# Due times that count each engine's queue, rests of splits written over the loaded tiles, and shorter pauses between the first operands of the up projection

## The chip, the cores and the metric

The kernel runs on one core of a Trainium2 chip. The metric is the device time of one execution in microseconds, as the median of several runs; lower is better. Five parts of the core matter here: TensorE (PE, matrix products and transposes by products with an identity), VectorE (DVE), ScalarE (ACT), the SyncE queue (SP) that hands out the transfers, and the DMA engines. GpSimd (POOL) does next to nothing.

## The reference

One layer of a decoder in fp32, for 2048 positions of 1024 features: two parallel groups of heads, cross-attention into 256 memory tokens, a gated feed-forward part, and norms between.

```python
h = rms_norm(x, mix_norm_g);  z = h @ w_in                      # 1024 -> 2048
lru_x, lru_gate, conf_a, conf_b = split(z, 4)
lru_x = causal_dwconv(lru_x, lru_conv_w, lru_conv_b)            # 4 taps
y_lru = rg_lru(lru_x, ...) * gelu(lru_gate)                     # gates, then a scan along positions
c = causal_dwconv(conf_a * sigmoid(conf_b), conf_conv_w, conf_conv_b)   # 31 taps
c = silu(layer_norm(c, conf_ln_g, conf_ln_b))
x = x + concat([y_lru, c]) @ w_out
h = rms_norm(x, xa_norm_g);  m = rms_norm(mem, mem_norm_g)
p = softmax((h @ w_q) . (m @ w_k) / 16)                         # 4 heads of 256
x = x + (p @ (m @ w_v)) @ w_o
h = rms_norm(x, ffn_norm_g);  g, u = split(h @ w_up, 2)         # 1024 -> 2 x 3072
x = x + (gelu(causal_dwconv(g, ffn_conv_w, ffn_conv_b)) * u) @ w_down
return rms_norm(x, final_norm_g)
```

## The kernel before

**Products.** Each fp32 operand of a product is split into two rounded parts: `hi`, a copy in a rounded format (ACT), and `lo`, the rest (DVE subtracts `hi` from the source). `mm3` (L603) then makes three matmuls of a 128x128 by 128x512 tile: hi by hi, lo by hi, hi by lo. The names in the profile are `xh/xl`, `yh/yl`, `Xh/Xl`, `hidh/hidl` and `wh/wl`. Larger products are made from seven block products in place of eight, with sums and differences of blocks (`S1` to `S4` on one side, `T1` to `T4` on the other): `seven` (L1129) with weights that `Quads` (L1078) prepares for the mixer's and attention's output products, `strassen_cols` (L1450) for the up projection, whose activations `HalfX` (L1388) holds, and `Down` (L1582 on) for the down projection, with weights from `prepare_down`.

**Stages.** Up to about 550 us: norms, memory, input projection and the convolutions. About 550 to 1090 us: for each half of the positions (`attend`, L1273) the recurrent gates, the product with w_out, attention (scores, exponentials of `prob`, transposes of it into `pt`, product into the residual `x1`), and the norm before the feed-forward part. From about 1090 us: the up projection, first for the positions of half 0, then (about 1550 us) half 1; then the down projection and the last norm.

**What sets the order.** Nothing is issued as it is written. The parts of the layer are generators; `drive` (L510) steps them by a clock that counts the recorded PE work, and a `yield n` pauses a generator for n us of that clock. They record operations (`Program.do`, `Program.dma`, L199 and L227), each with an engine, an estimated cost, predecessors, and the buffers that it touches. Tiles come from pools of slots: 85 of 128x512 (`S`), 4 and 3 wider ones, 8 banks of PSUM (`ps`), and a tile gets its slot when an earlier one has been let go. When all is recorded, `emit` (L403) plans up to three times: `deadlines` (L260) gives each operation a due time from an order of PE's work, and `schedule` (L281) walks through time, and on each engine issues, of the operations that are ready, the one with the earliest due time. The next pass takes its PE order from the last; the plan with the shortest estimate is issued, engine by engine, each engine in its planned order.

A due time before is that of the PE work behind it less the costs and hops of the chain between:

```python
for o in reversed(self.ops):
    lat = o.cost + o.delay + HOP
    for s in o.succs:
        o.due = min(o.due, s.due - lat)
```

It counts the chain of one operation, not what else stands on the engine. In a split, `lo` has its own slot (`pair`, L499; `split`, L595). `first_x` (L1785 on) makes the first four operands of the up projection, `X[0].make(key)`, with a pause of 20 behind each, and `feed_forward` starts when it has ended.

Of the kernel before, what the change touches and what calls it, by code (L numbers as in the profile page):

```python
# [11 lines left out]
F32 = mybir.dt.float32  # L12
# [5 lines left out]
P = 128  # L18
# [38 lines left out]
PASSES = 3  # L57

# [11 lines left out]
class Buf:  # L70


    def __init__(self, tag, shape, real=None, dtype=F32, name="t"):
        self.tag, self.shape, self.real, self.dtype, self.name = tag, tuple(shape), real, dtype, name
        self.ops, self.heads = [], []
# [24 lines left out]
class Ref:  # L100
    def __init__(self, buf, steps, dummy):
        self.buf, self.steps, self.dummy = buf, steps, dummy

    def __getitem__(self, i):
        return Ref(self.buf, self.steps + (lambda ap: ap[i],), self.dummy[i])

    def f32(self):
        return Ref(self.buf, self.steps + (lambda ap: ap.bitcast(F32),), self.dummy)
# [22 lines left out]
def resolve(a):  # L131
    return a.resolve() if isinstance(a, Ref) else a

# [13 lines left out]
class Program:  # L147
# [51 lines left out]
    def do(self, eng, name, out, *args, reads=(), writes=(), **kw):  # L199
        outs = [out] + ([kw["accum_out"]] if "accum_out" in kw else [])  # L200
        ins = [a for a in list(args) + list(kw.values()) if isinstance(a, Ref) and a not in outs]
        if eng == "PE":
            o = self.group or self.op("PE")
            n = ins[1].n if name == "matmul" else P
            if name == "matmul":
                rounded = ins[1].buf.dtype == F32R
                cost = (n + 32) / 2400.0 if rounded else n * 4 / 2400.0
            else:
                cost = 0.11
# [11 lines left out]
        o.calls.append((name, (out,) + args, kw))  # L221
        self.touch(
# [37 lines left out]
    def deadlines(self, order):  # L260
# [10 lines left out]
        for o in reversed(self.ops):  # L271
# [6 lines left out]
            if o.first:  # L278
                o.due = o.idx - 1e6

# [167 lines left out]
def hybrid_layer(  # L448
# [629 lines left out]
    class Quads:  # L1078
# [7 lines left out]
        def prepare(self, pace):  # L1086
            sub = ALU.subtract
            for i in range(KH):
# [5 lines left out]
                for n, t in enumerate((b11, b21, t2, t1, t3, t4, b22)):  # L1094
                    for j, b in enumerate(parts(t)):
# [30 lines left out]

    held = [0]

    def seven(order, L, W, add, amid):  # L1129
        banks, left = {}, {}  # L1130
# [4 lines left out]
        for n, (p, bank, start, outs) in enumerate(order):  # L1135
# [4 lines left out]
            for i in range(KH):  # L1140
                lh, ll = parts(L.get(akey, i))
# [246 lines left out]
    class HalfX:  # L1388
# [40 lines left out]
        def make(self, key):  # L1429
            sub = ALU.subtract  # L1430
            if key in self.t:
# [13 lines left out]
            for b in src:  # L1445
                hi, lo = pair("X")
                split(b[:], hi, lo)
                self.B[key].append((hi, lo))

    def strassen_cols(c0, B, outs, used=None):  # L1450
# [11 lines left out]
        def product(bank, src, key, start):  # L1462
            X = B.get(key)
            wh, wl = pair("w", (P, KQ, P))
            split(src, wh, wl)
# [25 lines left out]
        product(c, s1[:], "T1", True)  # L1491
        yield 0
        s3 = comb(a11, a21, ALU.subtract)
        product(a, s3[:], "T3", False)
# [8 lines left out]
        product(c, s4[:], "B22", False)  # L1503
# [54 lines left out]
    def prepare_down():  # L1558
        yield attends[NH - 1]
        for c in range(NCK):  # L1560
            for i in range(KD):
                f = c * 2 * KD + i
                raw = []
                for r0 in (f * P, (f + KD) * P):
                    for half in range(2):
                        t = tmp("wd")
                        pr.dma(t[:], w_down[0, r0 : r0 + P, half * TT : (half + 1) * TT])
                        raw.append(t[:])
                b11, b12, b21, b22 = raw
                t1 = combine("t", b12, b11, ALU.subtract)  # L1570
                t2 = combine("t", b22, t1[:], ALU.subtract)
                t3 = combine("t", b22, b12, ALU.subtract)
                t4 = combine("t", b21, t2[:], ALU.subtract)
# [236 lines left out]
```

## Time and profile before

| | |
|---|---|
| time, median of 3 runs | 2493.47 us (2490.45 to 2495.44) |
| the profiled execution | 2495.1 us |
| its span | 2493.3 us |
| its mean granted clock of TensorE | 0.988 |
| matmuls and transposes on PE | 10788 |
| ACT in the page | 2256 instructions |
| DMA | 572.07 MB, 229 GB/s over the span |

The time is that of the whole execution; the span runs from the first to the last instruction of the profile. All instructions are issued from one line of the recorder (L420, in the changed kernel L447), so that groups and rows are told apart by the names of their tiles, `out<-in`. A row of the timeline is start, duration, engine, line, operation, tiles and shape, a count `xN` where like rows follow each other, and in brackets how long the engine had been idle and what ended it. Durations of neighbours overlap: instructions are pipelined, so the pitch from start to start is what one costs.

### The profile page before, as it was taken

How to read it: one execution, taken by the hardware profiler on the slowest of the kernel's cores; microseconds unless marked ns; L12 is line 12 of the kernel's file. 1: busy time of each engine (PE TensorE's matmuls, PEld its weight loads, DVE VectorE, ACT ScalarE, POOL GpSimd, SP SyncE). 2: the span in 40 equal slices, each digit the busy share in tenths (PEclk: the TensorE clock that was granted, in tenths of full speed). 3: DMA queues.
4: the chain of work that ended last, by engine and by line, in shares of the span. 5: the costliest groups of instructions: out<-in, count | busy, mean ns of one | idle time of the engine just before them, and what ended most of it. 6: DMA issues, size and time to landing. Idle time of an engine off the chain costs nothing.

```text
span 2493.3 us, 32519 instructions
## 1 busy us (share of the span) xinstructions
PE 2421.8 (97%) x10788; PEld 1988.5 (80%) x10788; DVE 1921.3 (77%) x3187; ACT 1290.6 (52%) x2256; POOL 0.7 (0%) x6
## 2 busy tenths in 40 slices
PE   6999999999998999999999999999999999999998
PEld 5788868877767888878888887788888888888886
DVE  4579968999988645779888887987876775667665
ACT  8426668266977655775545455654443431233222
POOL 0000000000000000000000000000000000000000
PEclk8999999999999999999999999999999999999999
DMA  6987678797786966586654546644422288769774
GB/s 221 376 296 228 228 237 302 248 349 243 241 300 224 372 221 228 167 278 241 226 204 155 182 162 194 235 166 163 169 76 85 93 293 269 249 224 368 257 251 157
DMA packets 339839, 572.07 MB, mean 229 GB/s; under 512 B 32925, under 2 KB 106653, under 8 KB 339671
## 3 DMA queue, kind: packets, MB, share of 16 engines
q1 hardware_dynamic: 339670, 570.00, 67.0%
q8 instruction: 85, 1.39, 0.2%
q14 instruction: 84, 0.68, 0.1%
HBM read 385.32 MB, written 184.55 MB: 229 GB/s over the span
## 4 chain that ended last, share of the span: by engine, by line
PE 87%; DVE 5%; DMA 4%; ACT 3%; issue 1%; SPq 0%; DVEq 0%; ACTq 0%
PE ps L420 87%; ACT prob L420 1%; DVE yl L420 1%; DMA raw<-in_w_out_dram 1%; DVE t L420 1%; DMA VO<-VO 0%; DMA x<-in_x_dram 0%; DMA yf<-yf 0%; DVE s L420 0%; DVE prob L420 0%; DVE xc L420 0%; DVE gate L420 0%; ACT L420 0%; DVE Xl L420 0%; ACT x L420 0%
## 5 line engine op out<-in xcount | busy, mean ns | idle before, releaser
L420 PE MATMUL ps<-Xh,wl 128*128 128x512 f32 x1344 | 523.9, 390 | 2.5 <-DVE wl L420 2.5
L420 PE MATMUL ps<-Xh,wh 128*128 128x512 f32 x1344 | 524.3, 390 | 1.6 <-ACT wh L420 1.6
L420 PE MATMUL ps<-Xl,wh 128*128 128x512 f32 x1344 | 523.4, 389 | 0.0
L420 PEld LDWEIGHTS ps<-Xh,wl 128*128 128x128 f32 x1344 | 252.6, 188 | 57.1 <-DVE wl L420 4.7
L420 PEld LDWEIGHTS ps<-Xh,wh 128*128 128x128 f32 x1344 | 252.7, 188 | 55.3 <-ACT wh L420 2.9
L420 PEld LDWEIGHTS ps<-Xl,wh 128*128 128x128 f32 x1344 | 252.7, 188 | 52.1
L420 PE MATMUL ps<-wh,yh 128*128 128x512 f32 x672 | 268.9, 400 | 7.0 <-ACT pt L420 3.7
L420 PE MATMUL ps<-wh,yl 128*128 128x512 f32 x672 | 265.0, 394 | 4.9 <-DVE yl L420 4.9
L420 PE MATMUL ps<-wl,yh 128*128 128x512 f32 x672 | 264.5, 394 | 0.1
L420 PE MATMUL ps<-wh,hidh 128*128 128x512 f32 x672 | 261.4, 389 | 0.0
L420 PE MATMUL ps<-wl,hidh 128*128 128x512 f32 x672 | 261.4, 389 | 0.0
L420 PE MATMUL ps<-wh,hidl 128*128 128x512 f32 x672 | 261.4, 389 | 0.0
L420 DVE TENSOR_TENSOR acc<-acc,ps 128x512 f32<-128x512 f32 x192 | 129.5, 685 | 150.3 <-PE ps L420 149.9
L420 PE MATMUL ps<-xh,wh 128*128 128x512 f32 x512 | 201.8, 394 | 0.9 <-DMA wh<-w_in 0.8
L420 PE MATMUL ps<-xh,wl 128*128 128x512 f32 x512 | 199.5, 390 | 2.3 <-DVE wl L420 1.7
L420 PE MATMUL ps<-xl,wh 128*128 128x512 f32 x512 | 199.3, 389 | 0.0
L420 ACT ACTIVATE wh<-s 128x512 fp32r<-128x512 f32 x192 | 119.8, 629 | 136.5 <-DVE s L420 99.9
L420 PEld LDWEIGHTS ps<-wh,yh 128*128 128x128 f32 x672 | 128.0, 191 | 36.9 <-ACT pt L420 4.6
L420 PEld LDWEIGHTS ps<-wh,yl 128*128 128x128 f32 x672 | 127.9, 190 | 34.1 <-DVE yl L420 7.1
L420 DVE TENSOR_TENSOR wl<-s,wh 128x512 fp32r<-128x512 f32 x192 | 131.2, 688 | 27.3 <-ACT wh L420 25.4
L420 ACT ACTIVATE u<-ps 128x512 f32<-128x512 f32 x144 | 85.9, 597 | 126.5 <-PE ps L420 125.4
L420 PEld LDWEIGHTS ps<-wl,yh 128*128 128x128 f32 x672 | 128.2, 191 | 27.6 <-issue 0.8
(200 smaller groups left out, 4113.0 us busy)
## 6 DMA issues: line engine op xcount, KB each, us to landing
raw<-in_w_up_dram SPq DMA_DIRECT2D x96, 512.0 KB
wh<-w_down SPq DMA_DIRECT2D x164, 256.0 KB
wl<-w_down SPq DMA_DIRECT2D x164, 256.0 KB
hid<-cv SPq DMA_DIRECT2D x48, 512.0 KB
h<-hid SPq DMA_DIRECT2D x96, 256.0 KB
w_down<-wh SPq DMA_DIRECT2D x84, 256.0 KB
w_down<-wl SPq DMA_DIRECT2D x84, 256.0 KB
x<-in_x_dram SPq DMA_DIRECT2D x64, 256.0 KB
```

The lines of the kernel that those rows point to most:

```text
L420: getattr(e, name)(*[resolve(a) for a in args], **{k: resolve(a) for k, a in kw.items()})
```

## The change

Three parts, and no instruction of PE, DVE or SP is added or removed; ACT has three more table loads, since its functions stand in another order.

1. `deadlines` runs over each of DVE, ACT and SP twice (`STACKS`) behind the chain's due times: from the latest due operation of the engine back to the earliest, each is due no later than the next one's due time less its own cost, so that operations that compete for an engine push each other forward; then the chain's rule carries this to the predecessors.

2. A new `split_over` writes `lo` over the source tile itself, in place of a slot of its own. It does so where the source was written only by transfers or already rounded (`loaded`), and where the source isn't read any more; else it takes a slot as before. In `seven` the last uses are counted out by `last_uses`. In the profile such a rest reads as `raw<-raw,yh` where it read `yl<-raw,yh`.

3. `first_x` pauses for 5 in place of 20.

```diff
+STACKS = 2
...
+class Over:
+    def __init__(self, buf):
+        self.buf, self.dtype = buf, F32R
+    def __getitem__(self, i):
+        return self.buf[i].r()
...
         o.calls.append((name, (out,) + args, kw))
+        for r in outs:
+            if not r.rounded:
+                r.buf.loaded = False
...
             if o.first:
                 o.due = o.idx - 1e6
+        for _ in range(STACKS):
+            for e in ("DVE", "ACT", "SP"):
+                t = 1e9
+                for o in sorted((o for o in self.ops if o.eng == e and not o.first), key=lambda o: -o.due):
+                    t = o.due = min(o.due, t - o.cost)
+            for o in reversed(self.ops):
+                lat = o.cost + o.delay + HOP
+                if o.eng != "PE" and not o.first:
+                    for s in o.succs:
+                        o.due = min(o.due, s.due - lat)
...
+    def split_over(b, name):
+        hi, lo = rnd(name + "h", b.shape), Over(b) if b.loaded else rnd(name + "l", b.shape)
+        ACT(hi[:], b[:], AF.Copy)
+        V("tensor_tensor", lo[:], b[:], hi[:].f32(), op=ALU.subtract)
+        return hi, lo
...
-                    for j, b in enumerate(parts(t)):
+                    for j, b in enumerate(split_over(t, "y")):
...
-                lh, ll = parts(L.get(akey, i))
+                lh, ll = split_over(L.get(akey, i), "y") if n in spent else parts(L.get(akey, i))
...
-                hi, lo = pair("X")
-                split(b[:], hi, lo)
+                if self.h or key[0] == "T" or key == "B22":
+                    hi, lo = split_over(b, "X")
+                else:
+                    hi, lo = pair("X")
+                    split(b[:], hi, lo)
...
-        product(c, s1[:], "T1", True)
+        product(c, None, "T1", True, s1)
...
-                    hi, lo = pair("w")
-                    split(src, hi, lo)
+                    hi, lo = split_over(src, "w")
...
-                hi, lo = pair("hid")
-                split(src[:], hi, lo)
+                if akey in ("S1", "S3", "S4") or (akey == "A22" and not self.h):
+                    hi, lo = split_over(src, "hid")
+                else:
+                    hi, lo = pair("hid")
+                    split(src[:], hi, lo)
...
         for key in UP_ORDER[:EARLY]:
             X[0].make(key)
-            yield 20
+            yield 5
```

How this moves instructions is shown at three places.

DVE in the input projection, around 100 us; `wl<-raw,wh` is the rest of a tile of w_in that PE is to use next, `sg` the evacuation of its products, and `t` and `yl` are differences and rests of w_out, stored for much later. Before:

```order
L420 TENSOR_TENSOR yl<-t,yh 128x512
L420 TENSOR_TENSOR t<-raw 128x512
L420 TENSOR_TENSOR t<-raw,t 128x512
L420 TENSOR_TENSOR sg<-ps,sg 128x512
L420 TENSOR_TENSOR t<-raw,t 128x512
L420 TENSOR_TENSOR yl<-t,yh 128x512 x2
L420 TENSOR_TENSOR sg<-ps,sg 128x512
L420 TENSOR_TENSOR yl<-t,yh 128x512
L420 TENSOR_TENSOR yl<-raw,yh 128x512
L420 TENSOR_TENSOR wl<-raw,wh 128x512 x5
```

The changed kernel, at the same `sg` rows:

```order
L447 TENSOR_TENSOR yl<-t,yh 128x512
L447 TENSOR_TENSOR t<-raw,t 128x512
L447 TENSOR_TENSOR t<-raw 128x512
L447 TENSOR_TENSOR t<-raw,t 128x512
L447 TENSOR_TENSOR yl<-t,yh 128x512
L447 TENSOR_TENSOR raw<-raw,yh 128x512 x2
L447 TENSOR_TENSOR yl<-t,yh 128x512 x2
L447 TENSOR_TENSOR sg<-ps,sg 128x512 x3
L447 TENSOR_TENSOR wl<-raw,wh 128x512 x2
L447 TENSOR_TENSOR sg<-ps,sg 128x512
L447 TENSOR_TENSOR wl<-raw,wh 128x512 x2
```

Before, the `wl` rows stand behind the last `yl`; after, they follow the `sg` rows, and the `yl` and `t` rows between the `sg` rows have gone ahead of them or behind.

ACT at the first softmax, around 685 us; `prob,small<-prob,small` are the exponentials with their sums, `yh<-s` splits of the w_out product's left side. Before:

```order
L420 ACT_TABLE_LOAD
L420 ACTIVATE m<-m 128x512
L420 ACTIVATE yh<-s 128x512 x3
L420 ACT_TABLE_LOAD
L420 ACTIVATE prob,small_125<-prob,small_124,small_118 128x256
L420 ACTIVATE prob,small_128<-prob,small_127,small_118 128x256
L420 ACTIVATE prob,small_131<-prob,small_130,small_118 128x256
L420 ACTIVATE prob,small_134<-prob,small_133,small_118 128x256
L420 ACTIVATE prob,small_125<-prob,small_124,small_118 128x256
L420 ACTIVATE prob,small_128<-prob,small_127,small_118 128x256
L420 ACTIVATE prob,small_131<-prob,small_130,small_118 128x256
L420 ACTIVATE prob,small_134<-prob,small_133,small_118 128x256
```

The changed kernel:

```order
L447 ACT_TABLE_LOAD
L447 ACTIVATE m<-m 128x512
L447 ACT_TABLE_LOAD
L447 ACTIVATE prob,small_134<-prob,small_133,small_118 128x256
L447 ACTIVATE prob,small_131<-prob,small_130,small_118 128x256
L447 ACTIVATE prob,small_128<-prob,small_127,small_118 128x256
L447 ACTIVATE prob,small_125<-prob,small_124,small_118 128x256
L447 ACTIVATE prob,small_134<-prob,small_133,small_118 128x256
L447 ACTIVATE prob,small_131<-prob,small_130,small_118 128x256
L447 ACTIVATE prob,small_128<-prob,small_127,small_118 128x256
L447 ACTIVATE prob,small_125<-prob,small_124,small_118 128x256
L447 ACTIVATE yh<-s 128x512 x2
```

Three `yh<-s` stood between the square roots (`m<-m`) and the exponentials; now there is none, and two stand behind all eight exponentials.

PE at the start of the up projection, around 1088 us; `wh,yl` are the last matmuls of the attention's output, `ident,xn` transposes of the normalised rows of the second half of the positions, `Xh` and `Xl` the activations of the up projection. Before:

```order
L420 MATMUL ps<-wh,yh 128x512
L420 MATMUL ps<-wl,yh 128x512
L420 MATMUL ps<-wh,yl 128x512
L420 MATMUL ps<-ident,xn 128x128 x16
L420 MATMUL ps<-Xh,wh 128x512
L420 MATMUL ps<-Xl,wh 128x512
L420 MATMUL ps<-Xh,wl 128x512
```

The changed kernel:

```order
L447 MATMUL ps<-wh,yh 128x512
L447 MATMUL ps<-wl,yh 128x512
L447 MATMUL ps<-wh,yl 128x512
L447 MATMUL ps<-Xh,wh 128x512
L447 MATMUL ps<-Xl,wh 128x512
L447 MATMUL ps<-Xh,wl 128x512
```

The sixteen transposes are gone from here: 144 matmuls with `Xh` and `Xl` stand ahead of the first eight transposes, and the rest of them come between later products, eight or four at a time. On DVE the differences `t<-xn` and rests `Xl` of the first four operands move forward with them.

SP, not shown, hands out the reloads of w_in (`wh<-w_in`, `wl<-w_in`) around 500 us ahead of some stores of `A`, `z` and `gelu` which stood ahead of them.

More of the change, by code (lines that the diff above doesn't have):

```diff
@@ L74, in __init__ @@
         self.tag, self.shape, self.real, self.dtype, self.name = tag, tuple(shape), real, dtype, name
-        self.ops, self.heads = [], []
+        self.ops, self.heads, self.loaded = [], [], True
         self.free = int(np.prod(self.shape[1:]))
@@ L205, in do @@
             if name == "matmul":
-                rounded = ins[1].buf.dtype == F32R
-                cost = (n + 32) / 2400.0 if rounded else n * 4 / 2400.0
+                cost = (n + 32) / 2400.0 if ins[1].rounded else n * 4 / 2400.0
             else:
@@ L1125, in hybrid_layer, with last_uses, make @@
              ("P7", "a", False, [C21, C22]), ("P2", "a", True, [C11]), ("P3", "b", False, [C12]))
+    NEEDS = dict(S1=("A21", "A22"), S2=("S1", "A11"), S3=("A11", "A21"), S4=("A12", "S2"))
+    def last_uses(keys):
+        made, uses = set(), {}
+        def make(key, n):
+            if key in NEEDS and key not in made:
+                made.add(key)
+                for k in NEEDS[key]:
+                    make(k, n)
+                    uses[k] = n
+        for n, key in enumerate(keys):
+            make(key, n)
+        return [n for n, key in enumerate(keys) if uses.get(key, -1) <= n]
     held = [0]
     def seven(order, L, W, add, amid):
+        spent = last_uses([PRODUCTS[p][0] for p, _, _, _ in order])
         banks, left = {}, {}
@@ L1430, in make @@
             sub = ALU.subtract
+            assert not self.h or self.t or key[0] == "B"
             if key in self.t:
@@ L1460, in comb, with product @@
             return t
-        def product(bank, src, key, start):
+        def product(bank, src, key, start, over=None):
             X = B.get(key)
-            wh, wl = pair("w", (P, KQ, P))
-            split(src, wh, wl)
+            if over:
+                wh, wl = split_over(over, "w")
+            else:
+                wh, wl = pair("w", (P, KQ, P))
+                split(src, wh, wl)
             with together():
@@ L1490, in strassen_cols @@
         c = ps()
-        product(c, s1[:], "T1", True)
+        product(c, None, "T1", True, s1)
         yield 0
         s3 = comb(a11, a21, ALU.subtract)
-        product(a, s3[:], "T3", False)
+        product(a, None, "T3", False, s3)
         u3 = copied(a)
@@ L1502, in strassen_cols @@
         s4 = comb(a12, s2[:], ALU.subtract)
-        product(c, s4[:], "B22", False)
+        product(c, None, "B22", False, s4)
         outs(0, 1, u2, c)
@@ L1567, in prepare_down @@
                         pr.dma(t[:], w_down[0, r0 : r0 + P, half * TT : (half + 1) * TT])
[L1568 removed]
+                        raw.append(t)
                 b11, b12, b21, b22 = raw
[L1570 to L1573, printed above, removed]
[L1574 to L1576 removed]
+                t1 = combine("t", b12[:], b11[:], ALU.subtract)
+                t2 = combine("t", b22[:], t1[:], ALU.subtract)
+                t3 = combine("t", b22[:], b12[:], ALU.subtract)
+                t4 = combine("t", b21[:], t2[:], ALU.subtract)
+                for key, src in (("B11", b11), ("B21", b21), ("T2", t2), ("T1", t1), ("T3", t3), ("T4", t4), ("B22", b22)):
+                    hi, lo = split_over(src, "w")
                     at = wd_at(c, key, i)
```

11 lines of the change are left out of this document (7 added, 4 removed).

## The prediction

> **What bounds the kernel now.** I read the page first, then the table of windows, then PE's waits, then the timeline around each wait.
>
> ```profile
> PE 2421.8 (97%) x10788; PEld 1988.5 (80%) x10788; DVE 1921.3 (77%) x3187; ACT 1290.6 (52%) x2256; POOL 0.7 (0%) x6
> 550.00:600.00 50.00, 46.12 (x201) 36.99 (x200) 50.00 (x87) 30.10 (x49) 0.00 (x0) 0.97 0.81 267
> 650.00:700.00 50.00, 43.53 (x171) 32.38 (x170) 44.17 (x87) 46.29 (x85) 0.00 (x0) 0.90 0.80 268
> 700.00:750.00 50.00, 45.10 (x188) 34.42 (x187) 47.93 (x90) 35.39 (x72) 0.00 (x0) 0.97 0.91 327
> 750.00:800.00 50.00, 43.60 (x191) 35.50 (x190) 47.43 (x80) 41.25 (x88) 0.00 (x0) 0.90 0.63 207
> 1000.00:1050.00 50.00, 47.70 (x229) 39.87 (x228) 36.48 (x76) 39.65 (x98) 0.00 (x0) 0.97 0.54 174
> 1050.00:1100.00 50.00, 44.16 (x189) 36.04 (x188) 37.45 (x65) 31.22 (x68) 0.00 (x0) 0.91 0.83 284
> 1100.00:1150.00 50.00, 49.59 (x241) 41.18 (x241) 41.89 (x68) 38.77 (x65) 0.00 (x0) 0.99 0.63 219
> 1550.00:1600.00 50.00, 46.88 (x201) 36.93 (x200) 50.00 (x80) 35.25 (x59) 0.00 (x0) 1.00 0.74 254
> 1600.00:1650.00 50.00, 50.00 (x222) 41.44 (x221) 46.33 (x74) 26.59 (x41) 0.00 (x0) 1.00 0.56 190
> 2400.00:2450.00 50.00, 50.00 (x223) 41.40 (x222) 34.47 (x55) 12.07 (x21) 0.00 (x0) 1.00 0.72 243
> ```
>
> In a row of windows stand the stretch, then the busy time and count of PE, PEld, DVE, ACT and POOL, the granted clock, the DMA share and GB/s. PE is the bound: 97% busy, and from 1600 us to 2450 it has not one idle tenth (50.00 of 50 at both ends of that stretch, clock 1.00). A full window holds 222 matmuls of 512 columns, so one costs 50/222 = 0.225 us. The change alters no count of matmuls. All that it can win is PE's idle time and the stretches at half clock that follow the longer waits, and both lie before 1600 us. A window's clock of 0.90 is 10% of 50 us lost, 5.0 us; 0.97 is 1.5. Where PE idles DVE is at 44 to 50 of 50, so there a step's place in DVE's queue decides. The slots that the in-place rests free can win nothing after 1600; before it they count only through the order.
>
> ```profile
> PE ps L420 <- ACT prob L420: 6.1, 2, 5.3
> PE ps L420 <- ACT xn L420: 5.4, 1, 5.4
> ...
> PE ps L420 <- DVE sum L420: 4.1, 2, 3.2
> PE ps L420 <- DMA wh<-w_in: 0.8, 1, 0.8
> PE ps L420 <- DMA wl<-w_in: 0.6, 1, 0.6
> ```
>
> The waits are total, count and longest, in us. These and the single waits below are the ones that the new order touches; the others (memory tokens, x and gains at the start) keep their place in it, and the tail behind the last matmul is the same.
>
> **The change part by part.** The in-place rests cost nothing by themselves: the instruction has the same shape, only its output lies elsewhere, and the nearest row of a subtraction into its own input takes as long as one into a new slot:
>
> ```profile
> L420 DVE TENSOR_TENSOR acc<-acc,ps 128x512 f32<-128x512 f32 x192 | 129.5, 685 | 150.3 <-PE ps L420 149.9
> L420 DVE TENSOR_TENSOR wl<-s,wh 128x512 fp32r<-128x512 f32 x192 | 131.2, 688 | 27.3 <-ACT wh L420 25.4
> ```
>
> 685 against 688 ns: nothing. (A later reader of the raw tile could be delayed; none is left, since only its last use writes over it.) What remains is order, in seven places.
>
> (a) Around 105 us, second block of w_in columns.
>
> ```profile
> 102.44 0.69 DVE L420 TENSOR_TENSOR sg<-ps,sg 128x512 f32<-128x512 f32 x1
> 103.05 0.68 DVE L420 TENSOR_TENSOR yl<-t,yh 128x512 fp32r<-128x512 f32 x1
> 103.65 0.68 DVE L420 TENSOR_TENSOR yl<-raw,yh 128x512 fp32r<-128x512 f32 x1
> 104.25 1.89 DVE L420 TENSOR_TENSOR wl<-raw,wh 128x512 fp32r<-128x512 f32 x3
> 104.99 0.50 PE L420 MATMUL ps<-xh,wl 128*128 128x512 f32 x1 [1.72 <-DVE wl L420]
> ```
>
> PE waits 1.72 for a `wl` that stands behind `yl` rows of w_out, which nobody needs for some 2000 matmuls. Two stand between the last `sg` and it (2 x 0.60 = 1.2), more before. In the new order `wl` follows the `sg` rows directly. I take -1.4; bounds 0 (the loaded tile or `wh` is late instead) and -1.7.
>
> (b) Around 503 us SP hands out the w_in reloads 24 matmuls earlier (24 x 0.225 = 5.4 us), past stores of A, z and gelu that nothing waits for soon. The two DMA waits, 0.8 + 0.6, go: -1.4, bounds 0 and -1.4.
>
> (c) 550 to 600 us, recurrent gates and w_out product. Idle 50 - 46.12 = 3.9, clock 1.5. The queues ahead of each late step are as long as before, within one or two rows of 0.60. -1, bounds +1 and -5.4 (all of it).
>
> (d) 640 to 800 us, both softmaxes of the first half. Idle 6.5 + 4.9 + 6.4 = 17.8, clock 5.0 + 1.5 + 5.0 = 11.5.
>
> ```profile
> 685.55 0.79 PE L420 MATMUL ps<-wh,yl 128*128 128x512 f32 x1 [2.99 <-DVE yl L420]
> 685.74 0.60 ACT L420 ACTIVATE prob<-prob,small,small 128x256 f32<-128x256 f32 x1 [1.47 <-DVE small L420]
> 690.43 2.89 ACT L420 ACTIVATE prob<-prob,small 128x256 f32<-128x256 f32 x7
> 753.49 3.35 DVE L420 RECIPROCAL r<-r 128x512 f32<-128x512 f32 x1
> 757.57 4.23 PE L420 MATMUL ps<-ident,prob 128*128 128x128 f32 x16 [5.32 <-ACT prob L420]
> ```
>
> In the first softmax the eight exponentials, 690.43 - 685.74 = 4.7 us of ACT, now stand ahead of the last two `yh<-s` of which the next product needs one at once. They also began before (they waited 1.47 for `small`), so the product slips 3 to 4 us; but the probabilities are then ready when the transposes come, which gives back 0.8 (the wait that stands there now) to 4. In the second softmax the 3.35 us reciprocal `r`, which stood ahead of the four small reciprocals that the 5.32 wait needs, goes behind them, and 24 products stand ahead of the `sum,ones` matmuls that waited 3.2. -2 to -5 there. Net -2; bounds +6 (slips of 4 and 2, nothing back) and -10 (the 5.32 and the 3.2 go, with 1.5 of clock).
>
> (e) 1019 us, a softmax of the second half.
>
> ```profile
> 1016.67 0.60 ACT L420 ACTIVATE prob<-prob,small,small 128x256 f32<-128x256 f32 x1
> 1017.26 0.60 ACT L420 ACTIVATE prob<-prob,small,small 128x256 f32<-128x256 f32 x1
> 1018.42 2.04 ACT L420 ACTIVATE pt<-ps 128x512 f32<-128x512 f32 x4
> 1019.07 0.80 PE L420 MATMUL ps<-wh,yh 128*128 128x512 f32 x1 [2.30 <-ACT pt L420]
> 1019.66 0.63 PE L420 MATMUL ps<-wl,yh 128*128 128x512 f32 x1
> ```
>
> Three exponentials stand ahead of the `pt` copies before, eight after: 5 x (1017.26 - 1016.67) = 2.9 more, less an estimated 1 to 2, since four copies of probabilities (0.4 each) stand further up and ACT comes there earlier. +1 of wait and +1 of clock: +2, bounds 0 and +5 (2.9 and 2 of clock).
>
> (f) 1076 to 1125 us, start of the up projection. This is the largest term.
>
> ```profile
> 1087.52 0.39 PE L420 MATMUL ps<-wh,yl 128*128 128x512 f32 x1
> 1093.34 2.96 PE L420 MATMUL ps<-ident,xn 128*128 128x128 f32 x7 [5.43 <-ACT xn L420]
> 1080.60 3.69 DVE L420 TENSOR_TENSOR t<-xn,t 128x512 f32<-128x512 f32 x6
> ```
>
> Before, 16 transposes of the normalised second half of the positions stand next, and wait for its statistics. With the shorter pause the up projection of the first half is recorded ahead of them, and 144 `X` matmuls (144 x 0.225 = 32.4 us) stand ahead of the transposes. The 5.43, the 0.4 that the window from 1100 lacks, and the clock behind (0.91 and 0.99: 4.5 + 0.5 = 5.0) go: -10.8. What is late next is DVE: from the first `t<-xn` to the last rest `Xl` that the product on T3 needs the order has 59 DVE rows at (1084.21 - 80.60)/6 = 0.60, 35.4 us, against 141 matmuls x 0.225 = 31.7. So 3.7 us come back, spread over the first products. -7.1; bounds -10.8 (DVE has a lead) and -2 (the 3.7 falls in one piece and clocks down again for 5.0).
>
> On that last bound the Trainium skill speaks. The rows at 1019 show half speed right after a wait of only 2.30 us: a matmul of 512 columns takes 0.63 and 0.80 us there, against 0.39 at 1087. "TensorE: Matmul & The Clock Gate", Part 1, has the array fall to half rate after at least one idle window of about 3.4 us. By that rule the pieces here, none above 3.4, would cost no clock, and the bound -2 would be -7; by the row a piece of 2.3 can cost it, so I keep -2.
>
> (g) 1549 to 1566 us, change to the second half of the rows.
>
> ```profile
> 1551.70 0.50 PE L420 MATMUL ps<-Xh,wl 128*128 128x512 f32 x1 [1.35 <-DVE wl L420]
> ```
>
> The window from 1550 lacks 50 - 46.88 = 3.1 us of PE, this 1.35 the longest piece, with DVE at 50.00 of 50. The new order puts each `wl` one product (12 matmuls, 2.7 us) earlier, ahead of the splits of the new half. -2.3, bounds 0 and -3.1.
>
> Three more table loads (75 to 78) cost ACT 3 x 1.28 us, and ACT is 52% busy: nothing on PE, except where they stand inside (d), whose bounds hold one.
>
> ```profile
> 755.14 1.28 ACT L420 ACT_TABLE_LOAD   x1
> 756.43 0.69 ACT L420 ACTIVATE r<-ps,eps 128x512 f32<-128x512 f32 x1
> ```
>
> The page "ScalarE: Activation LUTs", section "What ACT_TABLE_LOAD costs", of the Trainium skill adds a drain of about 1.38 us to each; the next ACTIVATE here starts 0.01 behind the load, so the trace does not show it in front of work; by the page three would be an estimated 8 us of ACT instead of 4.
>
> Sum: -1.4 - 1.4 - 1 - 2 + 2 - 7.1 - 2.3 = -13.2 on the profiled execution's 2495.1 (span 2493.3), that is 2481.9. That execution lies 1.6 above the median of the runs, 2493.5, so on the median: **2480**.
>
> **The rivals.**
> - *The moves cancel* (same). (f) ends at -2, since its DVE backlog falls in one piece, (d) at +4, (c) and (g) at 0 and -1: -1.4 - 1.4 + 0 + 4 + 2 - 2 - 1 = +0.2, 2494. For it: DVE is at its limit wherever PE waits (50.00 of 50), so an earlier step makes another later. Against: (f) and (g) have work moved that has hundreds of matmuls to spare.
> - *Exponentials ahead of operands* (slower). Four softmax blocks each put eight exponentials, 4.7 us of ACT, ahead of a `yh` or `pt`. If all four delay PE in full and one new wait clocks it down (5.0), it is 18.8 + 5.0, less the 13.2 of the other five terms ((d) and (e) cancel in the forecast): +10.6, 2504. It decides from three in full (14.1 + 5.0 - 13.2 = +5.9). For it: the new order at 685 and 1019. Against: half of these exponentials already stood there and PE was waiting anyway.
> - *DVE's backlog dissolves* (larger gain). With (c) at -4 and (d) at -10, the rest as forecast: -24.2, 2469. For it: 21.7 us idle and 13.0 of clock lie there. Against: the number of DVE rows ahead of the late steps there hardly shrinks.
>
> **How the numbers follow.** The forecast has 0.58, the moves that cancel 0.19, the slower case 0.12, the larger gain 0.11. 0.2%, 5.0 us, is about what a measurement of this kernel can tell from no change. Faster is forecast and larger gain, 0.58 + 0.11 = 0.69; same 0.19; slower 0.12. Added as independent, the distances from value to bound give 10 us on each side (mostly (d) with 8 and (f) with 4 to 5): 2470 to 2490. To hold 8 in 10 it is widened to both neighbours, 2468 to 2494, which leaves out the slower case and the ends of the others.
>
> **What would show it.** (a): no `wl` wait at 105. (b): no w_in wait at 503. (d): the 5.3 for `prob` gone, a new `yl` or `yh` wait of 3 to 4 after 680. (e): the wait for `pt` near 1019 at 3 to 4. (f): no wait for `xn`, 1.00 of clock there, and small waits for `Xl` of about 3.7 together. (g): under 1 of `wl` and `wh` waits near 1550. After 1600 windows of 50.00. The prediction is wrong if (f) shows a new long wait, or if PE's idle time between 550 and 800 moves by more than 10.

## The result

| | before | changed |
|---|---|---|
| median | 2493.36 us (2490.45 to 2495.44, 4 runs) | 2479.55 us (2477.32 to 2480.82, 4 runs) |
| profiled execution, its span | 2495.1, 2493.3 | 2480.82, 2479.0 |
| ratio to before, 95% interval | | 0.994 (0.9926 to 0.9954) |

The change is worth 13.8 us on the medians and 14.3 in the profiled spans. (In the experiments below one execution of e5 and one of e9 took some two times as long as the others or more; the medians 2485.42 and 2483.38 include it, and without it are 2484.76 and 2483.16.) The page of the changed kernel has the same matmuls and, but for three more on ACT, the same counts:

```profile
PE 2411.2 (97%) x10788; PEld 1986.0 (80%) x10788; DVE 1915.0 (77%) x3187; ACT 1290.1 (52%) x2259; POOL 0.7 (0%) x6
```

Its windows, in the columns of the prediction's:

```profile
550.00:600.00 50.00, 45.46 (x197) 37.05 (x196) 49.14 (x82) 31.80 (x51) 0.00 (x0) 0.93 0.82 264
650.00:700.00 50.00, 40.35 (x161) 31.44 (x160) 42.92 (x82) 45.17 (x83) 0.00 (x0) 0.90 0.78 261
700.00:750.00 50.00, 41.31 (x181) 32.33 (x180) 45.72 (x85) 35.72 (x83) 0.00 (x0) 0.97 0.95 332
750.00:800.00 50.00, 49.50 (x223) 39.96 (x223) 49.09 (x83) 37.40 (x74) 0.00 (x0) 0.96 0.63 200
1000.00:1050.00 50.00, 46.56 (x218) 38.75 (x217) 32.87 (x63) 33.53 (x77) 0.00 (x0) 0.93 0.55 169
1050.00:1100.00 50.00, 48.69 (x214) 39.68 (x213) 44.18 (x74) 31.10 (x70) 0.00 (x0) 1.00 0.65 225
1100.00:1150.00 50.00, 49.09 (x232) 40.53 (x232) 37.17 (x65) 36.28 (x56) 0.00 (x0) 1.00 0.53 183
1550.00:1600.00 50.00, 50.00 (x220) 41.27 (x221) 50.00 (x83) 31.15 (x54) 0.00 (x0) 1.00 0.62 207
2400.00:2450.00 50.00, 50.00 (x222) 41.44 (x221) 31.36 (x50) 11.79 (x22) 0.00 (x0) 1.00 0.52 179
```

Better: 750, 1050 (clock 0.91 to 1.00) and 1550. Worse: 650 and 700 lost 3 to 4 us of PE time to waits, and 1000. Windows mislead a little here, since the work in them has slid by up to 15 us. PE's waits of the changed kernel (total, count, longest) have other names in front:

```profile
PE ps L447 <- ACT pt L447: 6.9, 3, 3.4
PE ps L447 <- DVE sum L447: 6.0, 1, 6.0
PE ps L447 <- ACT yh L447: 5.0, 2, 3.3
PE ps L447 <- ACT xa L447: 3.5, 1, 3.5
...
PE ps L447 <- DVE Xl L447: 1.2, 1, 1.2
...
PE ps L447 <- DVE gb L447: 0.9, 1, 0.9
...
PE ps L447 <- ACT prob L447: 0.7, 2, 0.5
PE ps L447 <- DVE wl L447: 0.5, 1, 0.5
```

The waits for `xn` (5.4), w_in (1.4) and most of those for `wl` (4.2) and `prob` (6.1) are gone; `pt`, `sum`, `yh` and `xa` have grown by 2 to 4 each.

To compare like with like I cut both traces by PE's matmuls, counted from the first, at counts where both have the same work behind them, and take the time from start to start. That is the loss of a stage with its half clock included, in us:

| stage (matmuls) | before at | before | changed | difference | forecast |
|---|---|---|---|---|---|
| start (to 300) | 0 | 84.7 | 82.9 | -1.8 | 0 |
| a (300 to 1000) | 85 | 158.4 | 156.0 | -2.4 | -1.4 |
| 1000 to 2130 | 243 | 255.3 | 256.5 | +1.1 | 0 |
| b (2130 to 2200) | 498 | 17.9 | 15.9 | -2.0 | -1.4 |
| 2200 to 2400 | 516 | 45.8 | 47.3 | +1.5 | 0 |
| c (2400 to 2650) | 562 | 59.6 | 60.6 | +1.0 | -1 |
| d, first softmax (2650 to 2960) | 622 | 78.3 | 80.4 | +2.1 | } -2 |
| d, second softmax (3080 to 3300) | 727 | 64.6 | 58.9 | -5.7 | } |
| e (4340 to 4500) | 1011 | 36.6 | 39.1 | +2.5 | +2 |
| f (4620 to 5300) | 1075 | 157.4 | 150.1 | -7.3 | -7.1 |
| g (6650 to 6950) | 1538 | 73.7 | 69.3 | -4.4 | -2.3 |
| behind the last matmul | 2482 | 11.4 | 12.5 | +1.1 | 0 |

The stages left out differ by less than 0.05. The column sums to -14.3, the spans' difference.

### The profile page after: what moved, and what is told of

The parts are those of the page before. It is cut to its first block, busy times and chain, and to the rows that moved or that the text cites. A ratio compares the mean times of both kernels' runs of the same rounds, so it can differ in the third digit from the quotient of the medians.

```text
span 2479.0 us, 32376 instructions
## 1 busy us (share of the span) xinstructions
PE 2411.2 (97%) x10788; PEld 1986.0 (80%) x10788; DVE 1915.0 (77%) x3187; ACT 1290.1 (52%) x2259; POOL 0.7 (0%) x6
## 4 chain that ended last, share of the span: by engine, by line
PE 68%; DVE 6%; ACT 3%; DMA 1%; issue 1%; SPq 0%; DVEq 0%; ACTq 0%
PE ps L447 68%; ACT prob L447 2%; DVE yl L447 1%; DVE s L447 1%; DVE t L447 1%; DVE gate L447 0%; DVE x L447 0%; DMA wh<-w_out 0%; DMA VO<-yh 0%; DVE Xl L447 0%; ACT yh L447 0%; DVE small L447 0%; DVE prob L447 0%; DVE xc L447 0%; DVE wl L447 0%
## 5 line engine op out<-in xcount | busy, mean ns | idle before, releaser
L447 PE MATMUL ps<-wh,hidl 128*128 128x512 f32 x624 | 242.7, 389 | 0.0
L447 PE MATMUL ps<-Xl,wh 128*128 128x512 f32 x576 | 224.3, 389 | 1.3 <-DVE Xl L447 1.2
L447 ACT ACTIVATE wh<-raw 128x512 fp32r<-128x512 f32 x176 | 108.3, 626 | 81.9 <-PE ps L447 43.0
L447 PE MATMUL ps<-xn,wh 128*128 128x512 f32 x384 | 149.4, 389 | 0.0
```

Source lines behind the costliest of these rows:

```text
L447: getattr(e, name)(*[resolve(a) for a in args], **{k: resolve(a) for k, a in kw.items()})
```

## The experiments

Twelve kernels. One table first, the differences to before in us, stage by stage as above (p is the pause, d the counted queues, o the rests over their sources). Left out are the stage from 2200 to 2400 (-0.5 to +1.6), the tail (at most +0.6 in these), and the stages that move by at most 0.5, but for e11's down projection (+4.4). The last rows are the median and that of before, measured along with it.

| stage | e1 p | e2 d | e3 o | e4 do | e5 op | e6 | e7 | e8 | e9 | e10 | e11 | e12 |
|---|---|---|---|---|---|---|---|---|---|---|---|---|
| start | -2.6 | -3.5 | -2.6 | -1.1 | -2.1 | -4.1 | -1.6 | -1.5 | -1.2 | -3.3 | -2.7 | -1.5 |
| a | 0.0 | -1.1 | +2.9 | -2.4 | +3.1 | -2.4 | -2.4 | 0.0 | -2.4 | 0.0 | -2.4 | -2.4 |
| 1000 to 2130 | +0.5 | +10.2 | 0.0 | +1.1 | -0.1 | +1.0 | +1.2 | +0.2 | +2.5 | +1.0 | +7.2 | +1.2 |
| b | +1.7 | -2.0 | -1.6 | -2.0 | -1.5 | -1.9 | -2.0 | -0.1 | +2.0 | 0.0 | -2.0 | -2.0 |
| c | -2.7 | -4.0 | -0.9 | +1.1 | -1.1 | +0.1 | +1.0 | -1.5 | -1.8 | +0.2 | -4.6 | -1.3 |
| d, first | +3.6 | +4.3 | +3.7 | +0.8 | +4.2 | +4.8 | +0.7 | +2.3 | +5.1 | +0.6 | +7.0 | +2.7 |
| d, second | -0.6 | -4.1 | +0.6 | -5.0 | -1.6 | 0.0 | -5.1 | +1.2 | -4.4 | 0.0 | +2.5 | -5.1 |
| e | +0.1 | +2.4 | +0.1 | +1.2 | 0.0 | -1.5 | +1.2 | +0.1 | +0.7 | +0.1 | +1.3 | +0.1 |
| f | -5.7 | +2.4 | -1.3 | -0.6 | -7.8 | -7.4 | +0.2 | -1.6 | -7.3 | -1.3 | -6.0 | -7.4 |
| g | +0.3 | 0.0 | -4.2 | -4.3 | -3.7 | -4.4 | 0.0 | -4.2 | -4.4 | 0.0 | +0.2 | -4.4 |
| median | 2489.7 | 2498.0 | 2491.9 | 2484.0 | 2485.4 | 2481.1 | 2490.2 | 2490.3 | 2483.4 | 2492.7 | 2496.3 | 2475.9 |
| before | 2493.3 | 2493.3 | 2493.3 | 2493.3 | 2494.2 | 2494.2 | 2494.2 | 2494.2 | 2493.8 | 2493.8 | 2493.8 | 2493.6 |

Such a table needs its noise first. e1 and e8 issue the same order as before until the up projection, e10 until the second softmax; yet at the start they differ from it by -2.6, -1.5 and -3.3, and e1 by -2.7, +3.6 and +1.7 in c, d first and b. The half-clock stretches fall elsewhere each time. So the profiled execution of before was unlucky at the start (all twelve lie below it there, and its run lies above the median), and a stage with a changeable clock is told only to about 3 us by one profile. In the same way e4 and e7 issue on PE the changed kernel's order until the up projection, and e12 does so too; on DVE and ACT e12 follows it up to 950 us and e4 and e7 up to 1040 us, so that they repeat its stages up to there. The stages a, f and g, where the columns fall into groups, are told well.

**Parts alone: e1 to e5.** e1 is the kernel before with the last hunk of the diff alone, e2 with the loop in `deadlines` alone, e3 with all rests over their sources (`STACKS = 0`, pause 20).

> The kernel before with the pause of 5 alone. Theory (each gain has its own place, and the up projection's start belongs to the pause): PE has no wait for xn near 1093 and no half clock behind it, some 3 us of small waits for DVE rests there, and nothing else moves: 7.3 us less than before, about 2486. Rival (the new due times or the free slots make room on DVE for it): the start of the up projection gains under 3 us here, about 2491, with waits for Xl of 5 us or more.

Measured 2489.65, ratio 0.9987 (0.9978 to 0.9997). PE's wait for `xn` is gone, f falls by 5.7, a, d second, e and g stay. But the median falls by only 3.6 where 7.3 was expected, for f as for the whole: alone, the pause leaves a wait of 1.8 for `wl` in f and a window (1100 to 1150) at 0.97, 1.5 us, which the other parts take away. The pause is what wins f; the rival falls.

> The kernel before with the due times that count the engines' queues, and nothing else. Theory: the waits at 105 (wl), 503 (w_in) and 1549 to 1566 (wl, wh) go, the softmaxes change as in the changed kernel (a new wait for yh at 686, the 5.3 for prob at 757 gone, the wait for pt at 1014 at 3.4), and the 5.4 for xn stays: about 7 us less than before, 2486. Rival (the slots that the rests no longer take let work and transfers start earlier): without them the gains at 503 and near 1549 are missing, and it is 2491 or more.

Measured 2498.00, ratio 1.0015 (1.0006 to 1.0025): slower than before. Theory and rival both missed the size. b and d second move much as in the changed kernel, a only half as far (a wait of 0.93 for `wl` is left), g is not there (the rival's point), and a new loss of 10.2 stands at 405 us:

```profile
404.94 0.79 PE L431 MATMUL ps<-xh,wh 128*128 128x512 f32 x1 [5.32 <-DMA wh<-w_in]
400.00:450.00 50.00, 44.33 (x184) 35.99 (x185) 46.79 (x74) 29.61 (x41) 0.00 (x0) 0.93 0.92 328
```

A reload of w_in came late, and PE lost 5.67 us of busy time and 3.5 to the clock (0.07 x 50). That other work, which the due times put first, holds the slots that the reload needs is an argument here; e7 tests it.

> The changed kernel without the new due times and with the pause of 20, so that only the rests over their sources remain. Theory: nothing is won, 2493 within 3. Rival (slots): the waits at 503 and 1549 to 1566 are gone here, 2487.

Measured 2491.86, ratio 0.9995 (0.9986 to 1.0005): within the theory's 3 us in the whole, but not in its parts. g falls by 4.2 with the rests alone and by 0.0 with the due times alone: in this stage the rival is right, and it is the rests (e8 tells which of them); that they act through the slots is what e11 speaks for.

> The changed kernel with the pause of 20. Theory: all of its gain but the 7.3 us at the start of the up projection, about 2487, and the 5.4 for xn with half clock behind it is back. Rival (the three parts only work together): the wait for xn is shorter than before, or other gains are missing too, and it is 2490 or more.

Measured 2484.02, ratio 0.9964 (0.9952 to 0.9977): f is as before (-0.6), the wait for `xn` is 4.7 there with half clock behind it, and the other gains are kept. The rival's 2490 did not come; but d and o do not add: alone they give +4.7 and -1.4, together -9.2.

```diff
-STACKS = 2
+STACKS = 0
```

> The changed kernel without the new due times. If the parts add, it has the pause's gain at the start of the up projection (5.7 us when alone) and the gain near 1549 to 1566 that the rests over their sources gave alone (4.2), and keeps the wait for wl at 105: 2491.9 - 5.7 = 2486. If the due times are needed for the up projection's start (it lost 7.3 with them and 5.7 without), its segment is between -5.7 and -4.

Measured 2485.42, ratio 0.9965 (0.9951 to 0.9979). f lost 7.8, without any counted queue; my bounds of -5.7 and -4 held for the pause alone and missed what the rests add. The whole is what adding the parts gave (2486). a is not won here (+3.1): that one belongs to the due times.

**Which slots: e7, e8, e11.** e7 is e4 with rests over their sources in `Quads.prepare` alone, e8 e3 with those of `HalfX.make` alone (the first line below; in e7 the name is `y`, and `seven` makes its rests in slots of their own); e11 is the changed kernel with 81 slots (the second).

```diff
-        hi, lo = rnd(name + "h", b.shape), Over(b) if b.loaded else rnd(name + "l", b.shape)
+        hi, lo = rnd(name + "h", b.shape), Over(b) if b.loaded and name in ("X",) else rnd(name + "l", b.shape)
...
-SLOTS = dict(S=85, W=4, D=3, ps=8)
+SLOTS = dict(S=81, W=4, D=3, ps=8)
```

> The new due times with the pause of 20, and rests over their sources only where the weights of w_out and of the attention's products are prepared. With the due times alone PE waited 5.3 us for a reload of w_in at 405 us, and nothing for it with all rests over their sources. Theory (the stage's 85 slots were all taken, and the weights' rests held those that the reload needed): the wait at 405 is gone, while the waits for wl and wh near 1549 to 1566, 3 us later in their place, are still there. Rival (another order by chance): the wait at 405 stays.

Measured 2490.15, ratio 0.9986 (0.9976 to 0.9996). As the theory has it: no wait at 405, and the one near 1549 as long as before. SP hands out that reload when PE has begun 1679 matmuls, in e2 when it has begun 1704: 25 x 0.225 = 5.6 us later, about the wait. The planner made a new order here too, and no trace tells whether it put the reload so late in e2 for want of a slot or by the due times of the stores ahead of it; that a wait for a reload is back at 402 with four slots fewer (e11) speaks for the slots. The first row is the window in which e2 had lost 5.67 of PE, the second e7's wait at the change of halves:

```profile
400.00:450.00 50.00, 50.00 (x222) 41.42 (x221) 48.23 (x76) 32.87 (x43) 0.00 (x0) 1.00 0.98 347
1546.41 0.50 PE L447 MATMUL ps<-Xh,wl 128*128 128x512 f32 x1 [1.35 <-DVE wl L447]
```

> The kernel before with rests over their sources only in the operands of the up projection. Theory (these hold most slots when the halves change, and the slots set when the next splits and reloads can start): the waits of 3.7 us near 1549 to 1566 fall below 1.5, as they did with all rests over their sources (0.4), and nothing before 1000 us moves but by the clock's phase; 2489 to 2491. Rival (it is the reused h tiles or the weights of the up projection): the waits near 1549 stay at 3 or more, 2493.

Measured 2490.34, ratio 0.9984 (0.9974 to 0.9995). g falls by 4.2, its waits from 3.7 to 0.4 us; the stages of one order with before (a, b, e) stay. The window, with DVE as full as before but PE's 46.88 now 49.59, and a row of DVE in it in which the rest goes over its source:

```profile
1550.00:1600.00 50.00, 49.59 (x217) 40.11 (x216) 50.00 (x80) 34.35 (x59) 0.00 (x0) 1.00 0.71 247
...
1550.36 1.28 DVE L447 TENSOR_TENSOR tx<-tx,Xh 128x512 fp32r<-128x512 f32 x2
```

> The changed kernel with 81 slots of 128x512 in place of 85. Theory (the in-place rests work by freeing slots): the waits for wl and wh near 1549 to 1566 come back in part or whole (1.5 to 3.7 us), or a wait for a reload comes up where the stage is full, and the whole is 2 to 8 us slower than the changed kernel, 2482 to 2488. Rival (the changed order does it, and slots are not scarce): within 2 us of the changed kernel.

Measured 2496.31, ratio 1.0007 (0.9997 to 1.0017): 16.8 us slower than the changed kernel, twice the most that I had given, and no better than before the change. Waits come up in several stages (a and b are as in the changed kernel), one of them in the down projection, where neither kernel has any (+4.4 behind matmul 6950):

```profile
402.56 0.80 PE L447 MATMUL ps<-xh,wl 128*128 128x512 f32 x1 [3.90 <-DMA wl<-w_in]
...
1558.22 0.67 PE L447 MATMUL ps<-Xh,wh 128*128 128x512 f32 x1 [2.04 <-ACT u L447]
...
2290.22 0.50 PE L447 MATMUL ps<-wh,hidh 128*128 128x512 f32 x1 [1.81 <-ACT hidh L447]
```

That is 4 us for each slot taken away on average (16.8 / 4), and as the planner makes a new order each time, it holds for these four together.

**What counting ACT's queue does: e6, e9, e10, e12.**

```diff
-            for e in ("DVE", "ACT", "SP"):
+            for e in ("DVE", "SP"):
```

> The changed kernel with the queues of DVE and SP counted, and ACT's not. Theory (counting ACT's queue is what puts the exponentials ahead of the operands of the next product): the wait for pt near 1014 is back at 2.3 us and the half clock behind it shorter (-1.2 to -2.5 there), the wait for yh of 3.3 at 686 is under 2, the gains at 105, 503 and 1549 stay; some 2 to 4 us less than the changed kernel, 2476 to 2478. Rival (the exponentials' place comes from DVE's reductions, which come earlier): both waits stay within 0.5 us of the changed kernel's, 2480.

Measured 2481.09, ratio 0.9949 (0.9933 to 0.9966). Half right: the wait for `pt` is 2.30 again, and e is 4.0 shorter than in the changed kernel, of which the wait is 1.1 and the rest half clock that is not there at all. But the second softmax's gain is gone, d second at 0.0:

```profile
758.13 1.09 PE L447 MATMUL ps<-ident,prob 128*128 128x128 f32 x3 [5.25 <-ACT prob L447]
...
1017.86 0.50 PE L447 MATMUL ps<-wh,yh 128*128 128x512 f32 x1 [2.30 <-ACT pt L447]
```

So counting ACT's queue wins the second softmax and loses at `pt`. (The wait for `yh` at 686 is under 2 as expected, but one of 6.5 for `prob` stands behind it.)

```diff
-                for o in sorted((o for o in self.ops if o.eng == e and not o.first), key=lambda o: -o.due):
+                for o in sorted((o for o in self.ops if o.eng == e and not o.first and o.sets != (0,)), key=lambda o: -o.due):
```

> The changed kernel, but the exponentials (and what else needs only their table) are left out when ACT's queue is counted, so that they keep the due times of their chain. Theory (the exponentials' own stacking makes them early, and counting the rest of ACT's queue is what brings the second softmax its gain): near 1014 five exponentials stand ahead of the pt copies in place of eight, three before the change, so that wait is between 2.3 and 3.4, and the segment of the second softmax keeps at least 3 of its 5.7 us; total 2476 to 2480. Rival (counting ACT's queue helps the second softmax through the exponentials themselves): the wait for prob near 757 is back at 5 us and that segment's gain is under 1, total 2481 to 2484.

Measured 2483.38, ratio 0.9956 (0.994 to 0.9973). The theory's places hold: five exponentials ahead, the wait for `pt` is 2.86, between 2.30 and 3.44, and d second keeps 4.4. The total missed by 3 and lies where the rival had it: a reload of w_in is 1.8 late at 503 (b is +2.0), and the first softmax waits 8.6 for `prob`.

> The kernel before, with the four reciprocals of 512 columns due 6 us later, so that on DVE they stand behind the four small reciprocals that the probabilities need. Theory (the 3.35 us reciprocal ahead of them makes PE's wait of 5.3 us for prob at 757): that wait falls to 2 or less, and the segment of the second softmax is 3 to 5 us shorter, unless the wait moves to what needs the reciprocal. Rival (the wait comes from the exponentials' late start on ACT): it stays over 4.

```diff
+        for o in self.ops:
+            if o.calls and o.calls[0][0] == "reciprocal" and o.calls[0][1][0].n == TT:
+                o.due += 6.0
```

Measured 2492.66, ratio 0.9997 (0.9987 to 1.0006), d second 0.0. The wait for `prob` falls only from 5.32 to 3.16, and a new one of 1.42 comes up for what needs the reciprocal (it stands where one of 1.08 for `pt` was). Neither theory: the 3.35 us instruction is 1 to 2 of the wait, and moving it alone is worth nothing:

```profile
745.63 3.38 PE L423 MATMUL ps<-sum,ones 128*128 128x512 f32 x4 [4.91 <-DVE sum L423]
...
754.94 3.38 PE L423 MATMUL ps<-ident,prob 128*128 128x128 f32 x12 [3.16 <-ACT prob L423]
...
759.74 1.11 PE L423 MATMUL ps<-ident,prob 128*128 128x128 f32 x4 [1.42 <-ACT r L423]
```

The longer wait for `sum` (3.23 in before's profile) is not the reciprocal's: e1 and e8, which issue before's order here, wait 4.88 and 4.90 for it, and 4.11 and 4.78 for `prob`. The rows of e1:

```profile
747.25 3.75 PE L420 MATMUL ps<-sum,ones 128*128 128x512 f32 x4 [4.88 <-DVE sum L420]
...
758.57 4.22 PE L420 MATMUL ps<-ident,prob 128*128 128x128 f32 x16 [4.11 <-ACT prob L420]
```

e12 takes ACT's queue into account only up to the second half's softmaxes; up to there the order on PE, DVE and ACT is the changed kernel's.

```diff
-                for o in sorted((o for o in self.ops if o.eng == e and not o.first), key=lambda o: -o.due):
+                for o in sorted((o for o in self.ops if o.eng == e and not o.first and (e != "ACT" or o.due < 850)), key=lambda o: -o.due):
```

> The changed kernel with ACT's queue counted only for operations that are due before 850 us of PE work, which leaves the order as it is up to the softmaxes of the second half of the positions; there three exponentials stand ahead of the four pt copies, as before the change, in place of eight. Theory (their place alone makes that wait): the wait for pt near 1014 falls from 3.4 to 2.3 us, the segment around it is 1.2 to 4 us shorter than in the changed kernel, every other segment is the same but for the clock's phase, and the median is 2476 to 2478.5. Rival (the wait comes with the whole new order of that stage): it stays at 3.4, and the median at 2479 to 2481.

Measured 2475.88 (2474.36 to 2477.14, 5 runs), ratio 0.993 (0.9916 to 0.9943): the fastest of all, 3.7 below the changed kernel, whose fastest run is 2477.32. The changed kernel first, then e12, at the last exponential ahead of the `pt` copies, the copies, and the matmul that needs them:

```profile
1012.87 0.59 ACT L447 ACTIVATE prob<-prob,small,small 128x256 f32<-128x256 f32 x1
...
1013.46 2.03 ACT L447 ACTIVATE pt<-ps 128x512 f32<-128x512 f32 x4
...
1014.09 0.79 PE L447 MATMUL ps<-wh,yh 128*128 128x512 f32 x1 [3.44 <-ACT pt L447]
```

```profile
1010.88 0.60 ACT L447 ACTIVATE prob<-prob,small,small 128x256 f32<-128x256 f32 x1
...
1011.47 2.03 ACT L447 ACTIVATE pt<-ps 128x512 f32<-128x512 f32 x4
...
1012.11 0.50 PE L447 MATMUL ps<-wh,yh 128*128 128x512 f32 x1 [2.30 <-ACT pt L447]
```

Five exponentials fewer ahead, the wait 1.14 shorter and e 2.4 shorter, the rest of it half clock: f, g, a and b are the same to 0.1. This shows by itself that the exponentials' place makes that wait. The half clock is another matter. e4 and e7 have the eight exponentials ahead and the same wait of 3.44, yet lose only 1.2 in e. The windows of the changed kernel and of e4 around the wait, and e4's wait:

```profile
1005.00:1035.00 30.00, 26.57 (x114) 21.69 (x113) 22.56 (x40) 20.34 (x49) 0.00 (x0) 0.89 0.58 177
```

```profile
1005.00:1035.00 30.00, 26.57 (x119) 21.82 (x118) 23.05 (x41) 21.04 (x49) 0.00 (x0) 0.94 0.58 186
...
1014.18 0.65 PE L447 MATMUL ps<-wh,yh 128*128 128x512 f32 x1 [3.44 <-ACT pt L447]
```

PE is idle alike; the clock is 0.89 in one and 0.94 in the other, 1.5 us of 30. So of the 3.7 the exponentials' place is shown to win 1.1; the rest may be the clock's phase.

## Why the prediction was right, point by point

The forecast was -13.2 on the profiled execution and 2480 on the median; 2479.55 came. That it came so near is in part luck: the seven terms measured -16.2 together, 3.0 more than forecast, and the stages that were put at nothing gave back 1.9. The terms one by one:

- **(a), -1.4 forecast, -2.4 measured.** Right in the mechanism: every kernel with counted queues wins it, none without; with the queues alone (e2) it is half, -1.1, so the slots of the rests have a part in it. Too small, since I priced a wait at its idle time. The matmul ahead of it starts at 102.88 and the late one at 104.99:

```profile
102.88 0.40 PE L420 MATMUL ps<-xl,wh 128*128 128x512 f32 x1
104.99 0.50 PE L420 MATMUL ps<-xh,wl 128*128 128x512 f32 x1 [1.72 <-DVE wl L420]
105.33 0.40 PE L420 MATMUL ps<-xh,wh 128*128 128x512 f32 x1
```

From start to start that is 2.11, some 1.89 over the usual 0.225, and the next follows after 0.34, 0.11 more: 2.0 for an idle time of 1.72. The profile counts idle from the modelled end of a matmul (0.40 behind its start), though the next would have started 0.225 behind it.
- **(b), -1.4 forecast, -2.0 measured.** The waits went, but e3 wins it without the due times (-1.6) and e9 loses it with them (+2.0): where SP hands out a reload differs from plan to plan. (The stage itself is told to no better than 1.7, e1's difference in before's order; the waits, 1.4 before and none after, are the firmer sign.)
- **(c), -1 forecast, +1.0 measured**, inside its bounds, and inside the noise of a stage in which the same order as before differs by 2.7 (e1) and the changed order gives +1.0, +1.1, +1.0 and -1.3 (e4, e7 and e12 the last three). Nothing can be said of it.
- **(d), -2 forecast, -3.6 measured; the step that failed.** I had the second softmax win because the reciprocal goes behind the four small ones and 24 products stand ahead of the `sum,ones` matmuls. The 5.32 for `prob` did go (0.5 is left), but the wait for `sum` did not: it is 5.96 where it was 3.23 (4.9 in e1 and e8, which have before's order, and 5.11 in e4, e7 and e12, which have the changed one). And e10 shows the reciprocal's place to be worth nothing alone.

```profile
748.76 3.78 PE L447 MATMUL ps<-sum,ones 128*128 128x512 f32 x4 [5.96 <-DVE sum L447]
```

PE's waits in the two softmaxes sum to 18.8 us where they were 17.8 (3.2 more in the first, 2.1 less in the second); the rest is clock: the windows from 700 and 750 lose 0.03 and 0.04 of 50 where they lost 0.03 and 0.10, 3.0 us less. e6 shows that the gain hangs on counting ACT's queue (0.0 without, -4.1 to -5.7 with, e11 apart); by which of the moved instructions is open. In the first softmax I had PE slip 3 to 4 us behind the exponentials. The 2.99 wait there is one of 3.28 for `yh`, and the stage's +2.1 lies within what e1 (+3.6, same order as before) shows as noise. Taken over the profiles that share an order, the first softmax does not move (+0.7 to +2.7 in the four of the changed order, 0 to +3.6 in the four of before's: before, e1, e8 and e10), and the second falls by about 5 (-5.0 to -5.7 against -0.6 to +1.2 in before, e1 and e8). So the term was nearer -5 than -2, all of it in the second softmax.
- **(e), +2 forecast, +2.5 measured.** The wait is +1.1 by the mechanism named; e12 shows it. The other 1.4 is half clock, which e4 and e7 do not have with the same wait (+1.2 in all): that the forecast had +1 for it is luck.
- **(f), -7.1 forecast, -7.3 measured.** The 5.43 and the half clock went, and DVE is late next, as forecast, in two pieces:

```profile
1099.75 0.50 PE L447 MATMUL ps<-Xl,wh 128*128 128x512 f32 x1 [1.20 <-DVE Xl L447]
1103.45 0.47 PE L447 MATMUL ps<-Xh,wh 128*128 128x512 f32 x1 [0.91 <-DVE gb L447]
```

These are 2.1 of idle time (2.7 with some 0.3 each for the restart) of the 3.7 forecast. The clock was mis-sized too. I took 5.0 for it from the windows, but the half clock there begins while PE still waits, and that time had been counted as the wait. The windows of before, cut at the end of the wait:

```profile
1090.55:1093.34 2.79, 0.00 (x0) 0.00 (x1) 2.79 (x7) 2.19 (x5) 0.00 (x0) 0.50 0.83 275
1093.34:1100.79 7.45, 7.04 (x23) 5.58 (x24) 4.95 (x9) 6.97 (x12) 0.00 (x0) 0.50 0.92 337
```

PE works for only 7.45 us at 0.50, a loss of 3.7. So 5.84 of idle time and 3.7 of clock went, and 2.2 of idle time (0.1 of it elsewhere in the stage) came: -7.3. A clock priced too high and a backlog priced too high cancelled, so that the figure agrees to 0.2 is luck; besides, the kernels that keep the old pause lie between -1.6 and +2.4 in this stage. The clock stayed at 1.00 through both pieces; the bound of -2 was not needed. (It put 3.7 in one piece, so the sentence that no piece there is above 3.4 did not fit it; with pieces of 1.20 and 0.91 the run does not test it.)
- **(g), -2.3 forecast, -4.4 measured.** The waits that I bounded at 3.1 by one window were 3.7 in all, with the restart of each on top. I gave the gain to the new order; e2, e3, e7 and e8 show that the due times have no part in it and the rests over the X tiles all of it; with 81 slots it is gone again (+0.2, e11).
- **What I left out.** A wait of 1.3 for `qt` at 244 (+1.1 with the stage) and one of 1.4 for `xl` at 535 (+1.5) are new. The first stands in e10 too (1.38), in the order of before, so it may be chance; the second stands in no kernel of the old order. With +1.1 behind the last matmul, which no experiment repeats, they are partly made up for by the start, whose -1.8 is noise.

Two sentences ahead of the terms were wrong. That DVE is at 44 to 50 of 50 wherever PE idles does not fit the prediction's own rows: in the windows from 1000 and 1050, where (e) and (f) lie, it is at 36.48 and 37.45, and ACT ends the waits there. And that the in-place rests count "only through the order" was too little. They save no instruction, but e2 without them is slower than before, and e11 shows that slots are scarce: four fewer take the whole gain. Of the rivals, the exponentials ahead of operands did act, in (e) with 1.1 of wait, not in the four blocks in full that would have turned the sign.

On the clock: the Trainium skill's rule ("TensorE: Matmul & The Clock Gate", Part 1: half rate after an idle window of about 3.4 us) would have no half clock behind 2.30 us. The traces have it behind the 2.30 of before and of e12 (and of e1, e3, e5, e8 and e10), and none behind the same wait in e6. The windows of before and of e6 around it:

```profile
1005.00:1035.00 30.00, 27.70 (x133) 23.05 (x132) 20.80 (x44) 26.04 (x69) 0.00 (x0) 0.94 0.49 160
```

```profile
1005.00:1035.00 30.00, 27.70 (x140) 23.18 (x138) 21.66 (x46) 26.37 (x67) 0.00 (x0) 1.00 0.55 175
```

PE is idle for 2.30 of 30 us in both, and the clock is 0.94 in one and 1.00 in the other. So a wait's length alone does not decide here; where it falls does too, which the same section's free-running window would explain. The traces show such a grid: the half-clock stretches of before begin at 581.97, 684.37, 1018.87 and 1090.55 us, 30, 98 and 21 times 3.413 us apart. The windows of before on both sides of one edge, then those of e6 on its own grid (its last stretch before them ends at 764.42, and 1017.0 is 74 such steps on):

```profile
1015.46:1018.87 3.41, 1.30 (x12) 1.06 (x10) 3.21 (x6) 3.41 (x10) 0.00 (x0) 1.00 0.74 204
1018.87:1022.28 3.41, 3.21 (x8) 2.54 (x9) 3.23 (x6) 3.41 (x11) 0.00 (x0) 0.50 0.47 172
```

```profile
1013.60:1017.00 3.40, 1.96 (x17) 1.67 (x15) 3.21 (x7) 3.40 (x9) 0.00 (x0) 1.00 0.60 207
1017.00:1020.40 3.40, 2.54 (x11) 2.12 (x12) 3.21 (x7) 3.40 (x11) 0.00 (x0) 1.00 0.52 155
```

Before's wait leaves PE idle for 2.1 of the 3.41 us ahead of the edge; e6's is cut in two, 1.4 and 0.9. How much idle time a stretch must hold is not shown beyond these two.

## What to carry to other kernels

A late engine's queue has to be read at the place of each wait: what stands ahead of the late instruction that nobody needs yet. Slots and order are one resource: an order that is better for the engines can be worse for the whole when it holds slots longer (+4.7 us here), and the last 4 slots of 85 were worth 17 us. When a planner makes the order anew, compare stage by stage at equal counts of work, with two kernels of equal order as the measure of noise, and let the best parts be joined: restricting one rule to the stage that it helps gave 3.7 us more, of which 1.1 is traced to it.

## What I had not expected of the hardware

The clock's phase makes a profile's stages differ by up to 3.6 us for one and the same order (e1 and e10 against before), more than most terms of such a change; the median of before moves much less, 2493.3 to 2494.2 in the five times it was taken. An idle time on PE costs about 0.3 us more than it shows, an estimate from the one wait at 105; if it holds for others, a wait of 0.3 costs twice what it shows.
